# Bias tables moved into the first feed-forward, places kept for the first value weights, and a reordered begin of the second feed-forward in an f32 hybrid layer

## The chip, the core and the metric

One program on one core of a Trainium2 chip. The time is the device time of one launch in microseconds; a kernel's figure is the median over its runs. The profile of one launch is shown beside it.

## The reference

One layer on 1024 tokens of width 1024, all in float32:

```python
h = swiglu(rmsnorm(x, ffn1_pre_g), w_gate, w_up, w_down)      # width 2816
x = x + 0.5 * rmsnorm(h, ffn1_post_g)
q, k, v = split(rmsnorm(x, mix_pre_g) @ w_qkv)                # 16 heads of 64
o_na  = neighbourhood_attention(q[:8], k[:8], v[:8], na_rel_bias)   # windows on a 16 x 64 grid
o_dil = dilated_mixture_attention(q[8:], k[8:], v[8:], t5_rel_bias) # three dilated windows
x = x + rmsnorm(concat(rmsnorm(o_na), rmsnorm(o_dil)) @ w_out, mix_post_g)
h = swiglu(rmsnorm(x, ffn2_pre_g), ...)
x = x + 0.5 * rmsnorm(h, ffn2_post_g)
```

Both attentions add a bias to their scores: the first one from `na_rel_bias` by row and column offset, with a large negative number outside the window; the second from `t5_rel_bias` by a bucket of the distance.

## The kernel before, in words

The large products go by Strassen-Winograd: each operand is cut in four quarters, sums of quarters are formed, and seven products of half size take the place of eight. Each of them is three matmuls per 128 x 128 x 512 tile (lines 262 to 264), because a float32 operand is split into a high and a low fp32r part: high x high, high x low, low x high. A split is a cast on ACT (`pw` L612, `whi` L355) and a subtraction on DVE (L613, `wlo` L356).

`PairGemm` computes two weight blocks (gate and up, or q and k) against the normalised tokens. An "early" block needs only the first half of the tokens: `ahead` computes its products A11 and A12 and stores the sums to DRAM (s1d, sgd). Later `run` does the rest of every block, the full blocks: S2, the previous block's A22, S1, S3 and S4, twelve matmuls times five, with A11 and A12 first where the block had not been early. For each block DVE forms sums of the raw weights (L443 to L445, the steps direct and second of `prepare`), and ACT and DVE split them. `Passes` computes the products in seven passes over smaller pieces (the two down projections and the values); every `fetch` loads, casts and splits two pieces of weights.

The stages, in order: first feed-forward (early blocks to 100 us, full blocks to 460, down passes to 682), the first two value passes (to 716), early QK blocks (to 770), the other value passes (to 834), full QK blocks (to 940), attention (to 1175), w_out (to 1252), second feed-forward (early blocks to 1322, full blocks to 1690, down passes to 1900).

PE's order is written out by hand: the program's text is PE's order. `plan(n, {tick: [...]})` gives small steps to n turns, and a turn comes every six or twelve matmuls. Such a step is `U(t)`, the transposes of token tile t: four 128 x 128 transposes in one "put" on PE (`trp`, L170), then a cast on ACT (L171) and a subtraction on DVE (L172), with two buffers for trp. Five puts belong to a tile of the second half of the tokens, where sums of quarters (`s`, L234) are transposed too. `Finish.rest` loads the residual tiles (L732, from POOL's queue) and adds to them (L735); the norms follow (L162 on ACT, L211 on DVE). Most of the order on the other engines comes from a list scheduler; `c.behind(f, engines)` keeps what f issues behind the last instruction so far of the engines named. Every engine works through its queue in order, and SP and POOL issue most of the DMA transfers.

`build_bias` fills three tables in DRAM between the value passes: `gab` (two tables of 8 heads, each row shifted by one; L785), `nb` (filled with the negative number, L788, then with rows of the stacked bias, L793), from a small product with the bucket table (`tabp`, L780, with its addition L781 and its store `tab<-lc`, L782). The stacked bias `stk` is loaded at the program's start. Attention reads the tables.

## Time and profile before

| | |
|---|---|
| median of 3 runs | 1921.62 us (1916.37 to 1922.28) |
| the profiled execution | 1922.76 us, span 1921.0 us |
| mean granted TensorE clock | 0.989 |
| PE busy | 1851.7 us (96%) |
| DVE, ACT, POOL busy | 1313.9, 799.8, 311.7 us |
| DMA | 400.96 MB, mean 209 GB/s |

A row of the profile's groups reads: line, engine, operation, output <- inputs, shapes, count, then busy time and mean duration of one, then idle time of the engine just before, and what ended most of it. In a table of waits, "PE trp L170 <- DVE x L172: 4.3, 2, 2.6" says that PE's instruction of line 170 began late for DVE's line 172 by 4.3 us in all, twice, at most 2.6 us. In a timeline the row begins with start and duration, and ends with the idle time before the instruction and its releaser in brackets. PEclk is the granted clock as a share of full speed, and the DMA share is the mean busy share of 16 DMA engines.

### The profile page before, as it was taken

Reading aid. Unit: us, or ns where it says so; the run is one execution under the profiler, and the core shown is the slowest. Engines: PE = TensorE matmul, PEld = TensorE weight load, DVE = VectorE, ACT = ScalarE, POOL = GpSimd, SP = SyncE. Lnnn points to the kernel's source line nnn. Section 1 sums busy time; section 2 is a strip of 40 time slices with the busy share of each in tenths; the row PEclk is TensorE's granted clock in tenths of the full one; section 3 lists DMA queues with packets and bytes.
Section 4 is the critical chain, followed back from the end, with each engine's and each line's share of the span. In section 5 each row is a group of like instructions: output and inputs, shape, how many; then the busy total and the mean of one; then the engine's idle time right before and its main releaser. Section 6 shows DMA issues by size and latency. Waiting matters only on the chain.

```text
span 1921.0 us, 25047 instructions
## 1 busy us (share of the span) xinstructions
PE 1851.7 (96%) x9044; PEld 1545.2 (80%) x9044; DVE 1313.9 (68%) x2205; ACT 799.8 (42%) x1287; POOL 311.7 (16%) x504
## 2 busy tenths in 40 slices
PE   5999999999999989999999999989999999999997
PEld 4788888888888867778799987777888888888886
DVE  5778777676565866548566775776788777654557
ACT  4522333334444545224477765453222333344332
POOL 2111111111000122342432310121111111110000
PEclk8999999999999999999999999999999999999999
DMA  6645465645986756866974642483456655476563
GB/s 237 223 159 188 170 222 216 222 167 197 327 273 200 273 193 205 292 198 197 313 265 142 212 159 88 155 301 136 159 192 241 215 195 210 159 275 212 198 229 133
DMA packets 162461, 400.96 MB, mean 209 GB/s; under 512 B 18001, under 2 KB 34561, under 8 KB 160289
## 3 DMA queue, kind: packets, MB, share of 16 engines
q1 hardware_dynamic: 112880, 224.62, 35.3%
q0 software_dynamic: 48592, 172.64, 24.8%
q10 hardware_dynamic: 864, 2.10, 0.3%
q8 instruction: 71, 1.16, 0.2%
q14 instruction: 54, 0.43, 0.1%
HBM read 274.84 MB, written 129.50 MB: 210 GB/s over the span
## 4 chain that ended last, share of the span: by engine, by line
PE 82%; DVE 6%; issue 5%; DMA 4%; ACT 2%; POOL 1%; SPq 0%; DVEq 0%; POOLq 0%; ACTq 0%
PE mmp L264 16%; PE mmp L262 16%; PE mmp L263 16%; PE accp L263 8%; PE accp L262 8%; PE accp L264 8%; PE po L992 3%; PE ptp L891 2%; PE sp L980 2%; PE trp L170 1%; PE po L1113 1%; DMA wraw<-in_wqk_dram 1%; PE sp L1100 1%; DMA x<-x 1%; DMA wraw<-in_wu_dram 1%
## 5 line engine op out<-in xcount | busy, mean ns | idle before, releaser
L262 PE MATMUL mmp<-x,whi 128*128 128x512 f32 (+1 forms) x1464 | 579.8, 396 | 7.6 <-ACT whi L355 3.6
L264 PE MATMUL mmp<-x,wlo 128*128 128x512 f32 (+1 forms) x1464 | 575.5, 393 | 1.0 <-DVE wlo L356 1.0
L263 PE MATMUL mmp<-x,whi 128*128 128x512 f32 (+1 forms) x1464 | 574.8, 393 | 0.5 <-DVE x L172 0.2
L262 PEld LDWEIGHTS mmp<-x,whi 128*128 128x128 f32 x1464 | 278.2, 190 | 67.0 <-ACT whi L355 4.2
L264 PEld LDWEIGHTS mmp<-x,wlo 128*128 128x128 f32 x1464 | 277.9, 190 | 62.3 <-DVE wlo L356 1.9
L263 PEld LDWEIGHTS mmp<-x,whi 128*128 128x128 f32 x1464 | 278.4, 190 | 59.9 <-DVE x L172 1.4
L613 DVE TENSOR_TENSOR pw<-praw,pw 128x1024 fp32r<-128x1024 f32 (+1 forms) x182 | 199.2, 1138 | 122.4 <-ACT pw L612 122.1
L612 ACT CAST pw<-praw 128x1024 fp32r<-128x1024 f32 (+1 forms) x182 | 169.2, 983 | 208.6 <-PE accp L264 168.0
L355 ACT CAST whi<-wraw 128x1024 fp32r<-128x1024 f32 x129 | 135.2, 1050 | 251.6 <-PE mmp L263 213.0
L262 PE MATMUL accp<-pw 128*128 128x512 f32 x600 | 234.4, 391 | 0.0
L264 PE MATMUL accp<-pw 128*128 128x512 f32 x600 | 233.5, 389 | 0.0
L263 PE MATMUL accp<-pw 128*128 128x512 f32 x600 | 233.4, 389 | 0.0
L356 DVE TENSOR_TENSOR wlo<-wraw,whi 128x1024 fp32r<-128x1024 f32 x129 | 157.6, 1225 | 23.6 <-ACT whi L355 23.5
L264 PEld LDWEIGHTS accp<-pw 128*128 128x128 f32 x600 | 112.6, 188 | 23.7
L262 PEld LDWEIGHTS accp<-pw 128*128 128x128 f32 x600 | 112.7, 188 | 23.5 <-issue 0.4
L263 PEld LDWEIGHTS accp<-pw 128*128 128x128 f32 x600 | 112.7, 188 | 23.0
L560 POOL DMA_DIRECT2D g<-sg x44 | 23.9, 542 | 475.2 <-DVE sg L553 304.0
L518 DVE TENSOR_TENSOR c<-mmp,u 128x512 f32<-128x512 f32 x52 | 36.0, 691 | 83.9 <-PE mmp L264 82.8
L374 ACT COPY s<-mmp 128x512 f32<-128x512 f32 x52 | 30.5, 587 | 147.3 <-PE mmp L264 145.7
L355 ACT CAST whi<-traw 128x512 fp32r<-128x512 f32 x52 | 32.3, 621 | 118.2 <-DVE traw L444 59.2
L172 DVE TENSOR_TENSOR x<-trp,x 128x512 fp32r<-128x512 f32 x84 | 57.2, 687 | 34.7 <-ACT x L171 34.7
L443 DVE TENSOR_TENSOR wraw<-wraw 128x1024 f32<-128x1024 f32 x52 | 63.6, 1224 | 24.2 <-DMA wraw<-in_wqk_dram 11.9
(230 smaller groups left out, 2699.8 us busy)
## 6 DMA issues: line engine op xcount, KB each, us to landing
praw<-g SPq DMA_DIRECT2D x70, 512.0 KB
wraw<-in_wg_dram SPq DMA_DIRECT2D x44, 512.0 KB
wraw<-in_wu_dram SPq DMA_DIRECT2D x44, 512.0 KB
tr<-in_wd_dram SPq DMA_DIRECT2D x44, 512.0 KB
g<-sg POOLq DMA_DIRECT2D x88, 256.0 KB, 4.1
ts<-tr POOLq DMA_DIRECT2D x22, 1024.0 KB, 4.7
praw<-ts SPq DMA_DIRECT2D x88, 256.0 KB
praw<-in_wd_dram SPq DMA_DIRECT2D x66, 256.0 KB
```

The source lines that it names most:

```text
L172: nc.vector.tensor_sub(lo, ps, hi.bitcast(F32))
L262: nc.tensor.matmul(out, ahi, bhi, start=start, stop=False, skip_group_check=go_on)
L263: nc.tensor.matmul(out, ahi, blo, start=False, stop=False, skip_group_check=go_on)
L264: nc.tensor.matmul(out, alo, bhi, start=False, stop=stop, skip_group_check=go_on)
L355: nc.scalar.copy(hi, raw)
L356: nc.vector.tensor_sub(lo, raw, hi.bitcast(F32))
L443: nc.vector.tensor_sub(r[:, 0:2], r[:, 1:3], r[:, 0:2])
L612: nc.scalar.copy(w[side][:, 0, :m], raw[:, :m])
L613: nc.vector.tensor_sub(w[side][:, 1, :m], raw[:, :m], w[side][:, 0, :m].bitcast(F32))
L891: c.nc.tensor.transpose(self.tps[:, j, :], self.probs[:, j * P:(j + 1) * P], c.ident)
L980: nc.tensor.matmul(out, lhs, keys[i], start=i == 0, stop=i == 1)
L992: nc.tensor.matmul(po[0][:, un * 2 + j], u.pt[:, 2 * j + t, :], rhs, start=t == 0, stop=t == 1)
```

## The change

Six things are done.

1. `build_bias` becomes `bias_steps`: the same tables, in pieces that are spread over the turns 0 to 19 of the first feed-forward's full blocks, one to six transfers a turn. `gab` goes by head (16 pieces of 256 KB), the filling of `nb` in 4 pieces of 384 KB; the loads of `stk` leave the program's start and come here too. Each step is held behind the last POOL and DVE instruction.
2. The first value pass has a place of its own (pool `pf`) and raw buffers (pool `pv`) that exist during the last down passes: its first weights are loaded at turn 13 there, and cast and split at turn 20. The first two passes take their pieces in groups of two rather than four, with a turn every six matmuls. Four tiles `vt` stand in place of two.
3. The early QK blocks 0, 3 and 6 take that place for their split weights, and their raw loads the same raw buffers. The split of block 0 is issued at turn 13 of the 16 turns of these value passes.
4. In the value passes behind the early QK blocks, the first weights of the full QK blocks are loaded and prepared one pass further back, behind the last DVE and ACT instructions so far.
5. In the full blocks that had been early, `direct` and `second` for the next block are held behind u of this block on DVE.
6. The second feed-forward has 11 early blocks instead of 10; the transposes of tiles 0 and 1 come one turn earlier; the split of the first early block is issued with the last turns of w_out, into a place in the residual tiles' pool.

The core of the diff (lines left out are marked by "..."):

```diff
@@ -402,13 +409,16 @@
...
-            if b + 1 not in self.w:
+            later = b == 1 and 3 in self.place
+            if b + 1 not in self.w and not later:
...
+            if later:
+                c.behind(lambda: self.split_left(b + 1), ACT, DVE)
...
@@ -479,10 +489,10 @@
                 self.mm(a, w[T2], 0, S2)
                 u2 = sp.tile([P, T], F32, tag="u2", name="u2")
                 nc.vector.tensor_add(u2, a, s1)
+                marks = c.marks(DVE, ACT)
                 if last:
                     last()
-                direct()
-                second()
+                c.after(marks, lambda: (direct(), second()))
                 a = self.bank()
                 self.mm(a, w[T1], 0, S1)
                 v = sp.tile([P, T], F32, tag="v", name="v")
@@ -584,29 +594,44 @@
...
+    def __init__(self, c, n, left, right, take, last=None, first=None):
...
-        self.groups = [groups] * 6 + [last or groups]
+        self.groups = [first or groups] * 2 + [groups] * 4 + [last or groups]
...
             self.groups[0] = [groups[0][:2], groups[0][2:]] + groups[1:]
         self.todo = deque((p, g[j:j + 2]) for p in range(7) for g in self.groups[p] for j in range(0, len(g), 2))
...
+        self.ready, self.places, self.loaded, self.raws = deque(), deque(), deque(), None
+    def load(self, raw):
+        p, ids = self.todo[len(self.loaded)]
+        for j, i in enumerate(ids):
+            self.c.nc.sync.dma_start(raw[:, j], self.right(i)[PASSES[p][1]])
+        self.loaded.append(raw)
...
+        p, ids = self.todo[0]
...
+        if self.places:
+            w = [self.places.popleft()()]
+            if not self.loaded:
+                self.load(self.raws.tile([P, 2, T], F32, tag="raw", name="praw"))
+        self.todo.popleft()
...
+            loaded = bool(self.loaded)
+            raw = (self.loaded or raws).popleft() if self.loaded or raws else c.pw.tile([P, 2, T], F32, tag="raw",
+                                                                                       name="praw")
...
+            elif not loaded:
...
@@ -763,35 +788,65 @@
...
+def bias_steps(c, rel, t5, onehot, lncount, bp):
+    nc, g = c.nc, c.nc.gpsimd
...
+    def load(i):
...
+        g.dma_start(kept["oh"][:32, :511], onehot[:, cols])
+        g.dma_start(kept["lc"][:8, :511], lncount[:, cols].broadcast_to([8, 511]))
+    def begin():
+        c.bp = bp()
...
+        g.dma_start(kept["t5"], t5.rearrange("h b -> b h"))
...
+        g.memset(kept["neg"], NEG)
+        load(0)
+    def table(i):
+        oh, lc = kept["oh"], kept["lc"]
...
+        g.dma_start(tab[i, :, :511], lc[:8, :511])
+        if i == 0:
+            load(1)
+    def shift(h, i):
...
+        dst = bass.AP(tensor=x.tensor, offset=x.offset + h * P * 640, ap=[[641, P], [1, 511]])
+        g.dma_start(dst, tab[i, h:h + 1, :511].broadcast_to([P, 511]))
+    def fill(h):
+        g.dma_start(c.nb[h:h + 2].rearrange("h p r e -> p h (r e)"),
+                    kept["neg"].unsqueeze(1).broadcast_to([P, 2, 384]))
+    def shifted(cc):
+        g.dma_start(stk[cc], rel[:, :, 7 - cc:31 - cc])
+    def rows(r):
...
+        g.dma_start(c.nb[:, r * 8:r * 8 + 8, r0:r0 + 8, :].rearrange("h c r e -> c h (r e)"),
+                    stk[:, :, r0 - r + 7:r0 - r + 15, :].rearrange("c h r e -> c h (r e)"))
+    at = {0: [begin], 1: [lambda: table(0)], 2: [lambda: table(1)]}
...
+    for n in range(4):
+        add(n, fill, 2 * n)
+    for n in range(8):
+        add(n + 1, shifted, n)
+        for i in range(2):
+            add(2 * n + i + 4, shift, n, i)
+            add(n + 9, rows, 2 * n + i)
+    return {k: [lambda f=f: c.behind(f, POOL, DVE) for f in fs] for k, fs in at.items()}
...
@@ -1237,8 +1292,8 @@
...
-        def one_a_turn(steps, n, first):
-            plan(n, {first + i: [f] for i, f in enumerate(steps)})
+        def one_a_turn(steps, n, first, more):
+            plan(n, {i: steps[i - first:i - first + 1] * (i >= first) + more.get(i, []) for i in range(n)})
...
@@ -1284,11 +1340,13 @@
...
-            one_a_turn(sums, NF, NF - 3 - len(sums))
+            bt = sub()
+            one_a_turn(sums, NF, NF - 3 + (which == 3) - len(sums), tables(pool, bt))
...
+                bt.close()
...
@@ -1329,7 +1387,7 @@
...
-                          9: [lambda: fin.rest([2, 3], hs.get)], 10: [U(1)], 17: [U(2)], 19: [U(3)]})
+                          9: [lambda: fin.rest([2, 3], hs.get)], 10: [U(1)], 17: [U(2)], 19: [U(3)], **tail(prep, op)})
...
@@ -1415,34 +1473,57 @@
...
+            def values_ahead(stack, op):
+                vp.append(Passes(c, 4, op, getv, vearly, first=[[0, 1], [2, 3]]))
...
+                def place():
+                    return first.tile([P, 1, 2, 2, T], F32R, tag="w", name="pw")[:, 0]
+                def load():
...
+                    vp[0].places.append(place)
...
+                    for i in range(2):
+                        vp[0].load(raws.tile([P, 2, T], F32, tag="raw", name="praw"))
+                return {13: [load], 20: [lambda: vp[0].fetch()]}
+            op, fin, hs, prep = ffn(1, op0, prep, gate_pairs(1, op0, a["wg1"], a["wu1"], 9), get1,
+                                    {0: [F(4, 5), L(6, 7)], 2: [U(4)], 3: [F(6, 7), U(5)], 5: [U(6)], 6: [U(7)]},
+                                    down_sums(a["wd1"], ts1), value_sums(a["wv"], tsv),
+                                    a["ffn1_post_g"], a["mix_pre_g"], x0, x1, begin,
+                                    lambda pool, e: bias_steps(c, a["na_rel_bias"], a["t5_rel_bias"], a["onehot"],
+                                                               a["lncount"], lambda: pool("bp", 1, e)), values_ahead)
+            qkv, w, e = sub(), sub(), sub()
+            c.xb = pool("xb", 1, qkv)
+            op.second()
+            vp, = vp
+            pr, c.vt = pool("pr", 2, e), pool("vt", 1, e)
+            vp.places.extend([lambda: pr.tile([P, 1, 2, 2, T], F32R, tag="w", name="pw")[:, 0]] * 3)
+            for i in range(4):
+                vts.append(c.vt.tile([P, 4 * VW], F32, tag=f"v{i}", name="vt"))
+                nc.gpsimd.memset(vts[i].rearrange("p (h f) -> p h f", f=65)[:, :, 64:65], 1.0)
...
+            pg.place = {b: lambda: early[0]().rearrange("p h m x -> h p m x") for b in (0, 3, 6)}
+            plan(16, {0: [lambda: fin.scale(4, 4), A(4, 5)], 9: [lambda: queued(pg.start)], 10: [U(4)],
+                      13: [lambda: c.behind(lambda: pg.split_left(0), DVE, ACT)]})
...
+            early_pools(e, 2, 2)
...
@@ -1460,12 +1540,12 @@
...
-            pg.fetch(0)
-            pg.fetch(1)
-            build_bias(c, a["na_rel_bias"], a["t5_rel_bias"], a["onehot"], a["lncount"])
-            vp.run(4, 5)
-            pg.begin()
-            pg.begin_rest()
+            queued(lambda: pg.fetch(0))
+            vp.run(4)
+            queued(lambda: pg.fetch(1))
+            c.behind(pg.begin, DVE, ACT)
+            vp.run(5)
+            c.behind(pg.begin_rest, DVE, ACT)
...
@@ -1600,7 +1680,9 @@
             p2, g3 = prep_pool(prep, [(a["mix_post_g"], "post"), (a["ffn2_pre_g"], "pre")])
             left_pool(prep, side="right")
             op = Operand(c, g3, 2)
-            pg = gate_pairs(3, op, a["wg2"], a["wu2"], 10)
+            pg = gate_pairs(3, op, a["wg2"], a["wu2"], 11)
+            pg.place[0] = lambda: c.xp.tile([P, 2, 2, T], F32R, tag="s", name="w0", bufs=c.deep).rearrange(
+                "p h m x -> h p m x")
             fin = Finish(c, x1, x2, p2, op)
             hs = [part, hs1p.tile([P, 4, D], F32, name="hs")]
             A = lambda *ts: lambda: fin.rest(ts, lambda t: hs[t // 4][:, t % 4, :])
@@ -1621,8 +1703,8 @@
...
-            plan(12, {0: [lambda: fin.scale(0, 4), A(0, 1)], 3: [A(2, 3)], 5: [U(0)], 6: [U(1)],
-                      8: [lambda: queued(pg.start)], 9: [U(2)], 10: [U(3)]})
+            plan(12, {0: [lambda: fin.scale(0, 4), A(0, 1)], 3: [A(2, 3)], 4: [U(0)], 5: [U(1)],
+                      7: [lambda: queued(pg.start)], 9: [U(2)], 10: [U(3), lambda: pg.split_left(0)]})
...
```

Three places show how the order moves. First, DVE at full QK blocks 0 and 1 (`u` and `c` with the lower numbers are block 0's). Before:

```order
L481 TENSOR_TENSOR u_6581<-mmp,s_6566 128x512
L356 TENSOR_TENSOR wlo<-traw,whi 128x512
L444 TENSOR_TENSOR traw<-wraw 128x512
L445 TENSOR_TENSOR wraw<-wraw,traw 128x512
L489 TENSOR_TENSOR v<-mmp,u_6581 128x512
L356 TENSOR_TENSOR wlo<-wraw,whi 128x1024
L481 TENSOR_TENSOR u_6659<-mmp,s_6644 128x512
L356 TENSOR_TENSOR wlo<-traw,whi 128x512
L510 TENSOR_TENSOR c_6618<-mmp,v 128x512
L810 TENSOR_TENSOR k<-mmp,u_6581 128x512
```

With the change:

```order
L491 TENSOR_TENSOR u_6587<-mmp,s_6572 128x512
L453 TENSOR_TENSOR wraw<-wraw 128x1024
L454 TENSOR_TENSOR traw<-wraw 128x512
L455 TENSOR_TENSOR wraw<-wraw,traw 128x512
L499 TENSOR_TENSOR v<-mmp,u_6587 128x512
L363 TENSOR_TENSOR wlo<-traw,whi 128x512
L520 TENSOR_TENSOR c_6624<-mmp,v 128x512
L363 TENSOR_TENSOR wlo<-wraw,whi 128x1024
L865 TENSOR_TENSOR k<-mmp,u_6587 128x512
L890 TENSOR_TENSOR qk<-k,qk 128x512
L491 TENSOR_TENSOR u_6665<-mmp,s_6650 128x512
L453 TENSOR_TENSOR wraw<-wraw 128x1024
```

The first c has moved from behind the second u to ahead of it, and the preparation (L443 before, L453 now) of the next weights stands behind u.

Second, POOL in the first two value passes (`vs` and `v` are where the values are stored, `x` the residual tiles). Before, the load of tiles 6 and 7 and what stands ahead of it:

```order
L1436 DMA vs_5324<-vt 128x520
L1433 MEMSET vt 128x8
L1436 DMA vs_5324<-vt 128x520
L1433 MEMSET vt 128x8
L732 DMA x<-in_x_dram 128x1024 x2
L1070 DMA v_87<-vt 8x8x520 x2
```

With the change:

```order
L1516 MEMSET vt 128x8 x4
L220 DMA xn_2_4842<-xn 128x1024
L220 DMA xn_3_4843<-xn 128x1024
L757 DMA x<-in_x_dram 128x1024 x2
L761 DMA x_4_97<-x 128x1024
L761 DMA x_5_98<-x 128x1024
L1483 DMA vs_163<-vt 128x520 x4
L757 DMA x<-in_x_dram 128x1024 x2
```

The fills of vt with ones are all ahead of the first store; the loads of tiles 6 and 7 (the last row) stand behind the four stores of the first pass, as before.

Third, DVE at the end of the early blocks of the second feed-forward, where the last tiles are transposed (L172 before, L178 now). Before:

```order
L172 TENSOR_TENSOR x_11247<-trp,x_11246 128x4x128
L137 TENSOR_SCALAR v<-ss 128x2
L443 TENSOR_TENSOR wraw<-wraw 128x1024
L138 TENSOR_SCALAR y<-v 128x2
L172 TENSOR_TENSOR x_11239<-trp,x_11238 128x4x128
L139 TENSOR_SCALAR y<-y 128x2
L356 TENSOR_TENSOR wlo<-graw,whi 128x1024
L146 TENSOR_TENSOR e<-y,v 128x2
L172 TENSOR_TENSOR x_11241<-trp,x_11240 128x4x128
L147 TENSOR_TENSOR e<-e,y 128x2
L172 TENSOR_TENSOR x_11243<-trp,x_11242 128x4x128
```

With the change:

```order
L240 TENSOR_TENSOR s<-x_11811,s 128x512
L178 TENSOR_TENSOR x_11258<-trp,x_11257 128x4x128
L178 TENSOR_TENSOR x_11250<-trp,x_11249 128x4x128
L178 TENSOR_TENSOR x_11252<-trp,x_11251 128x4x128
L178 TENSOR_TENSOR x_11254<-trp,x_11253 128x4x128
L178 TENSOR_TENSOR x_11256<-trp,x_11255 128x4x128
L453 TENSOR_TENSOR wraw<-wraw 128x1024
L454 TENSOR_TENSOR traw<-wraw 128x512
L455 TENSOR_TENSOR wraw<-wraw,traw 128x512
```

The preparation of the first full block stood among the subtractions of the last two tiles; now it stands behind all of them.

87 lines of the change are left out of this document (32 added, 55 removed).

## The prediction

> **What bounds the kernel now.** I read the page's engine shares first, then stretches of the span with PE's busy time and granted clock, then PE's waits in the three stretches where it is short, then the rows of the engines that it waits for.
>
> ```profile
> PE 1851.7 (96%) x9044; PEld 1545.2 (80%) x9044; DVE 1313.9 (68%) x2205; ACT 799.8 (42%) x1287; POOL 311.7 (16%) x504
> ```
>
> The next engine, DVE, is busy for 68%; PE sets the time, with 1851.7 of the 1921.0 us. The diff keeps its matmuls, so it can win only the 69 us in which PE is idle and the stretches in which its clock is low. The stretches (span, PE busy, ..., clock, DMA share):
>
> ```profile
> core 0: us, PE busy (x) PEld busy (x) DVE busy (x) ACT busy (x) POOL busy (x), PEclk, DMA share, GB/s
> 100.00:240.00 140.00, 140.00 (x613) 114.99 (x613) 110.68 (x147) 35.34 (x44) 17.79 (x32) 1.00 0.53 175
> 682.00:728.00 46.00, 35.79 (x161) 26.60 (x160) 30.86 (x59) 21.76 (x36) 12.46 (x27) 1.00 0.62 213
> 810.00:818.00 8.00, 7.29 (x20) 5.79 (x21) 3.46 (x5) 0.00 (x0) 1.15 (x3) 0.59 1.02 250
> 850.00:854.00 4.00, 4.00 (x13) 3.09 (x12) 1.15 (x2) 1.46 (x2) 1.54 (x2) 0.59 0.31 99
> 1294.00:1298.00 4.00, 3.70 (x13) 3.03 (x14) 3.79 (x14) 0.60 (x2) 0.00 (x0) 0.57 0.43 128
> 1318.00:1326.00 8.00, 6.52 (x23) 5.37 (x24) 5.58 (x9) 1.76 (x3) 0.00 (x0) 0.57 0.23 82
> ```
>
> In the first row, full gated blocks, PE has no gap, so there is nothing to win there and something to lose. The second loses 46.00 - 35.79 = 10.2 us at full clock. In the other four PE runs at little over half clock; busy time times (1 - clock) is what that costs: 7.29 x 0.41 = 3.0, 4.00 x 0.41 = 1.6, 3.70 x 0.43 = 1.6 and 6.52 x 0.43 = 2.8 us. Each follows a gap. PE's waits in three windows (682 to 728, 806 to 855, 1235 to 1326; us in total, times, longest):
>
> ```profile
> PE trp L170 <- DVE x L172: 4.3, 2, 2.6
> PE accp L263 <- DVE pw L613: 2.0, 3, 1.0
> PE mmp L262 <- ACT whi L355: 1.7, 1, 1.7
> PE accp L262 <- ACT pw L612: 1.5, 2, 0.8
> PE mmp L264 <- DVE wlo L356: 0.5, 1, 0.5
> ...
> PE accp L263 <- DVE pw L613: 3.0, 1, 3.0
> PE mmp L262 <- DVE c L510: 2.0, 1, 2.0
> ...
> PE trp L170 <- DVE x L172: 8.6, 6, 3.4
> PE mmp L262 <- ACT whi L355: 1.8, 1, 1.8
> PE mmp L264 <- DVE wlo L356: 0.5, 1, 0.5
> ```
>
> Sums: A, first value passes, 10.0. B, end of the value passes and first two QK blocks, 5.0 and clock 3.0 + 1.6: 9.6. C, w_out to the end of the second feed-forward's early blocks, 10.9 and clock 1.6 + 2.8: 15.3. Together 34.9 us, all in the reach of the diff. The start, the turn into attention and the tail hold the other half of the idle time; the diff leaves them.
>
> **A, first value passes.** What PE waits for, on DVE, ACT and POOL:
>
> ```profile
> 703.10 1.09 POOL L732 DMA_DIRECT2D x<-in_x_dram  x2 [0.73 <-DVE s L234]
> 707.22 1.28 DVE L735 SCALAR_TENSOR_TENSOR x<-hb,y,x 128x1024 f32<-128x1024 f32 x1 [3.44 <-DMA x<-in_x_dram]
> 711.34 0.66 PE L170 MATMUL trp<-ident,s 128*128 128x128 f32 x4
> 697.27 0.59 ACT L1434 COPY vt<-accp 128x512 f32<-128x512 f32 x1 [3.04 <-DMA vs<-vt]
> ```
>
> The weight waits (2.0 + 1.5) have two reasons: the first pair is split only when the down passes have ended, and ACT's next cast stands behind a copy into vt that waits 3.04 us for a store, since vt has two buffers. Now the first pair has places of its own and is cast during the last down pass, half of a pass's weights is enough to begin, and four vt tiles end the copy's wait. I take 3.5 off. The QK split (1.7 + 0.5) stands behind the last copy of the passes; it moves to turn 13 of 16, with its load behind a raw buffer that comes free at the second split, some 20 us ahead of need. 2.2 off, 0.4 kept, as its two casts and subtractions end close to PE's arrival.
>
> The waits for a transposed tile (2.6, 1.8) are DVE's subtraction L172 behind L735, which waits for tile 6's load. In the new order the first subtraction is ahead of that addition, but the second is behind it. So the fourth transpose is gated where the third was. It arrives about 706.7: 711.34 before, less the 6.0 us of stalls ahead of it (3.5 for weights, 2.6 for the third transpose), plus six matmuls (140.00 us over 613, 0.23 each). The load goes 0 to 2.5 us before 703.10, as the two weight splits, about 1.2 us each, no longer stand before its release; it landed 4.1 us after issue (707.22), and 1.28 for the addition and 0.7 for the subtraction follow, so the tile is free between 706.7 and 709.2. That keeps 0 to 2.5 us; I take the middle, 1.3, having no row nearer to either end. The 1.8 had a split behind a late load ahead of it, which now lands earlier: 0.3 kept. A: **10.0 less 2.0 = 8.0** (4.9 where 2.5, 1.8 and 0.8 stay, 9.3 where no tile is waited for).
>
> **B, bias tables out of the value passes.** DVE here, with the DMA issues of 770 to 840 (KB each, us to landing):
>
> ```profile
> gab<-tab POOLq DMA_DIRECT2D x2, 2044.0 KB, 19.0
> nb<-neg POOLq DMA_DIRECT2D x1, 1536.0 KB, 8.3
> tab<-lc POOLq DMA_DIRECT2D x2, 16.0 KB, 6.8
> ...
> 807.09 1.23 DVE L443 TENSOR_TENSOR wraw<-wraw 128x1024 f32<-128x1024 f32 x1 [5.89 <-DMA wraw<-in_wqk_dram]
> 809.43 1.22 DVE L613 TENSOR_TENSOR pw<-praw,pw 128x1024 fp32r<-128x1024 f32 x1
> 847.58 0.69 DVE L481 TENSOR_TENSOR u<-mmp,s 128x512 f32<-128x512 f32 x1 [3.38 <-PE mmp L264]
> 848.78 0.68 DVE L510 TENSOR_TENSOR c<-mmp,v 128x512 f32<-128x512 f32 x1
> ```
>
> L443 waits 5.89 us for gated weights that share the engines (share 1.02) with 5.6 MB of bias; the split L613 that PE needs is queued behind it. Now the bias is gone from here and L443 stands behind four of the last splits, so either change alone would free PE. The 2.0 us gap is c of block 0 queued behind u of block 1, which waits 3.38 us for a product PE had yet to make; in the new order c is ahead. I keep 0.5 for the shorter queue. B: **9.1** (3.6 where the first gap and its clock, 6.0, stay; 9.6 where nothing does).
>
> What the bias costs in its new place: two small matmuls and additions, moved with PE's sum unchanged; the loads have one block of 13.7 us (60 matmuls) for landings of which the longest here, at a full DMA, was the 6.8 of tab. One chain is longer: the second lc load waits for the first tab store, so DVE's second addition may stand 0 to 2 us. PE would see that only past the slack of 3.1 us worked out under the slower rival; I charge 0.3. The pieces are one to six a block and hold POOL about half a microsecond each (x32 in 17.79 us of the 140), and their 6.4 MB over 20 blocks of at least 13.7 us are under 25 GB/s, at a DMA share of 0.53. What hides them is PE's own queue of products; were that cover gone, a block would be as much longer as its slowest piece is late.
>
> **C, second feed-forward's begin.** DVE and PE rows, the last from the first feed-forward:
>
> ```profile
> 1228.77 2.48 DVE L211 SCALAR_TENSOR_TENSOR xn<-x,y,gain 128x1024 f32<-128x1024 f32 x2
> 1231.73 0.60 PE L170 MATMUL trp<-ident,xn 128*128 128x128 f32 x4
> 1292.34 1.23 DVE L443 TENSOR_TENSOR wraw<-wraw 128x1024 f32<-128x1024 f32 x1 [4.05 <-DMA wraw<-in_wu_dram]
> 86.58 0.66 PE L170 MATMUL trp<-ident,s 128*128 128x128 f32 x4 [1.07 <-DVE x L172]
> ```
>
> The 10.9 are 1.5 at the transposes of U0 and U1 near 1237 and 1239, 2.3 at the first split, 3.4 at 1294 and 3.7 at the last seven puts (1316 to 1321). U0 goes one turn (12 matmuls, 2.75 us) earlier: it arrives about 1229.0, and the first half of L211 ends at 1230.0, so 1.0 to 1.1 us of wait takes the place of 1.5. The first split is placed two thirds into the last w_out turns instead of behind them: 2.3 off. L443 no longer stands before the last transposes: 3.4 and its clock loss of 1.6 off. An eleventh early block gives the seven puts that ended in a burst six matmuls each, all but the last three; a burst of three is what the first feed-forward ends with, and it waits 1.07. So of 3.7 + 2.8, 1.1 stays. C: **15.3 less 2.2 = 13.1** (7.7 where the burst and its clock stay, 14.2 where the last three puts wait for nothing). The eleventh block saves no matmul; its extra store and reload are 1 MB off PE's path.
>
> **Sum.** 8.0 + 9.1 + 13.1 - 0.3 = 29.9 off the profiled execution's 1922.76 us gives 1892.9; the median of the runs is 1.1 lower than that execution, so 1891.8: **1892 us**. The three low ends (16.2, less 0.3) give 1906, the high ones (33.1) 1888; the start, where eight small loads leave POOL ahead of the first tiles' stores, I put at nothing.
>
> The clock terms rest on rows: clock 0.59 behind gaps of 3.0 and 2.0 us, though the 2.6 us gap of A left it at 1.00. [...]
>
> **The rivals.** *The stalls pass on*: tile 6's load and the splits stay gates. Then A keeps 4.3 + 2.2, and C keeps its burst's 3.7 + 2.8 because transposes that come earlier find DVE just as full: 13.0 against the 3.1 that I keep there, so 1902. For it: most of the waits above name a subtraction queued on DVE, which is left 68% busy. Against it: behind 2.6, 3.0 and 3.4 of them stands a DMA wait (3.44, 5.89, 4.05) whose instruction is moved. *The loads are late without the bias too*, as the DMA share stays 1.02 in the row of 810 to 818, where the pieces of bias are only a part: B keeps its first gap and clock, 3.0 + 3.0, hence 1898. Against: 5.6 MB leave, and L443 stands further back. [...] *The change doesn't act*, schedulers refilling what is won: within 5 us of 1921.
>
> *Slower: DVE's new order in the early full blocks.* The preparation of the next weights (L443 and two more) was hoisted ahead of u; now it is held directly behind u, ahead of c and of the split needed three products later.
>
> ```profile
> 105.89 1.22 DVE L443 TENSOR_TENSOR wraw<-wraw 128x1024 f32<-128x1024 f32 x1
> 109.42 0.68 DVE L481 TENSOR_TENSOR u<-mmp,s 128x512 f32<-128x512 f32 x1
> ...
>   DMA wraw<-in_wu_dram: 11.4, 9
> ```
>
> From the end of u's product: u 0.7, the preparation 1.2 + 0.7 + 0.7, c 0.7, the split 1.2 (as L613 above): 5.2 us, against three products of 12 matmuls, 36 x 0.23 = 8.3, to the one that needs it. Slack 3.1. A DMA wait in front of L443 now hits that split, and cancels the gain if it costs PE 29.9 / 28 = 1.07 us in each of the 28 early full blocks, a wait of 4.2 us; at 4.7 us the time is 1892 + 28 x 1.6 = 1937. For it: DVE is busy 110.68 of 140. Against it: L443 moves 4 us later (behind 109.42 + 0.68, from 105.89), and in its early place it waited 11.4 us in all for these loads, 4.05 of them at 1292.
>
> **How the numbers follow.** My forecast 0.60 (its own range 1886 to 1899), stalls pass on 0.18, loads late 0.08, clock 0.03, doesn't act 0.06, slower 0.05. The range 1885 to 1909 takes in the first four and the low ends, with 3 us at either side for what the sum leaves out. A measurement tells 0.3% (6 us) from no change: faster 0.89, same 0.06, slower 0.05.
>
> **What would show it.** PE without waits over 0.5 us and clock 1.00 from 790 to 850 (B); one wait of about 1 us at a transpose in A, and two of about 1 us in C; no 8 us stretch of clock 0.57 before the second gated blocks; PE without idle time in the early full blocks. Idle time there, or a wait of DVE for wraw in every block, would be the slower rival; a 2 us wait for c, or half clock near 810, proves my B wrong.

## The result, and the profile after

The changed kernel takes **1899.96 us** in the median of four runs (1898.66 to 1901.49), the kernel before, timed beside it, 1921.95 (1916.37 to 1922.31). The ratio is 0.9899, with a 95% interval of 0.9877 to 0.9921; by the medians it is faster by 22.0 us, where 29.9 were forecast. The profiled execution took 1899.15 us (span 1897.0, mean granted clock 0.994), 23.6 less than that of before.

PE's line of the page, and the six stretches of the prediction's first table, after:

```profile
PE 1842.2 (97%) x9044; PEld 1538.3 (81%) x9044; DVE 1316.3 (69%) x2207; ACT 794.9 (42%) x1285; POOL 320.7 (17%) x519
```

```profile
core 0: us, PE busy (x) PEld busy (x) DVE busy (x) ACT busy (x) POOL busy (x), PEclk, DMA share, GB/s
682.00:728.00 46.00, 43.04 (x206) 34.39 (x205) 36.73 (x76) 24.30 (x44) 12.24 (x22) 1.00 0.63 211
810.00:818.00 8.00, 8.00 (x37) 6.64 (x36) 5.39 (x6) 2.95 (x3) 3.21 (x7) 1.00 0.38 117
850.00:854.00 4.00, 4.00 (x19) 3.33 (x18) 3.93 (x7) 1.57 (x2) 0.84 (x2) 1.00 0.71 201
1294.00:1298.00 4.00, 4.00 (x23) 3.32 (x22) 4.00 (x7) 2.32 (x5) 1.08 (x2) 1.00 0.17 66
1318.00:1326.00 8.00, 8.00 (x37) 6.54 (x36) 5.74 (x9) 1.67 (x2) 0.54 (x1) 1.00 0.43 154
100.00:240.00 140.00, 138.36 (x599) 111.51 (x599) 110.97 (x148) 34.65 (x44) 30.66 (x55) 1.00 0.59 196
```

The first row lost 10.2 us before and loses 46.00 - 43.04 = 3.0 now. The four stretches at half clock are gone. Only the last row is worse: PE had no gap in the early full blocks and now has one. PE's waits after, from the windows 100 to 460, 455 to 682, 678 to 735, 1205 to 1326 and 1440 to 1480 (us in total, times, longest); the window 806 to 855 has none:

```profile
PE mmp L268 <- DVE v L499: 1.6, 1, 1.6
...
PE accp L269 <- DVE pw L638: 1.0, 2, 0.6
...
PE mmp L270 <- DVE wlo L363: 1.7, 1, 1.7
PE trp L176 <- DVE x L178: 1.3, 1, 1.3
...
PE trp L176 <- DVE x L178: 2.5, 4, 1.3
PE trp L176 <- DVE xn L217: 0.9, 1, 0.9
...
PE mmp L268 <- DVE v L499: 2.5, 1, 2.5
```

What is left of A is 1.7 + 1.3 = 3.0, of B nothing, of C 2.5 + 0.9 = 3.4. Two places are new: a wait for `v` in each feed-forward, 1.6 + 2.5 = 4.2 us, and 1.0 us in the first feed-forward's down passes. So A won 10.0 - 3.0 = 7.0, B 9.6 and C 15.3 - 3.4 = 11.9, and 4.2 + 1.0 went back: 23.3 of the 23.6 us by which the profiled executions differ. The miss to be explained is the new waits (the two for `v` and those of the down passes), and some 2 us of more waiting in A and C than was allowed.

### The profile page after: what moved, and what is told of

It is laid out like the page before. It is cut to its first block, busy times and chain, and to the rows that moved or that the text cites. A ratio compares the mean times of both kernels' runs of the same rounds, so it can differ in the third digit from the quotient of the medians.

```text
span 1897.0 us, 25061 instructions
## 1 busy us (share of the span) xinstructions
PE 1842.2 (97%) x9044; PEld 1538.3 (81%) x9044; DVE 1316.3 (69%) x2207; ACT 794.9 (42%) x1285; POOL 320.7 (17%) x519
## 4 chain that ended last, share of the span: by engine, by line
PE 84%; DVE 6%; DMA 4%; issue 3%; ACT 2%; POOL 0%; SPq 0%; DVEq 0%; ACTq 0%; POOLq 0%
PE mmp L268 16%; PE mmp L270 16%; PE mmp L269 16%; PE accp L269 8%; PE accp L268 8%; PE accp L270 8%; PE po L1047 3%; PE ptp L946 2%; PE sp L1035 2%; PE trp L176 1%; PE po L1168 1%; PE sp L1155 1%; DMA tsv<-tr 1%; DMA sgd<-sg 1%; DMA gain<-in_ffn_pre_g_dram 0%
## 5 line engine op out<-in xcount | busy, mean ns | idle before, releaser
L268 PE MATMUL mmp<-x,whi 128*128 128x512 f32 (+1 forms) x1432 | 565.8, 395 | 6.5 <-DVE v L499 4.2
L270 PE MATMUL mmp<-x,wlo 128*128 128x512 f32 (+1 forms) x1432 | 561.2, 392 | 1.7 <-DVE wlo L363 1.7
L269 PE MATMUL mmp<-x,whi 128*128 128x512 f32 (+1 forms) x1432 | 560.7, 392 | 0.5 <-DVE x L178 0.2
L268 PEld LDWEIGHTS mmp<-x,whi 128*128 128x128 f32 x1432 | 271.1, 189 | 67.2 <-issue 6.5
L270 PEld LDWEIGHTS mmp<-x,wlo 128*128 128x128 f32 x1432 | 271.0, 189 | 61.0 <-DVE wlo L363 2.4
L269 PEld LDWEIGHTS mmp<-x,whi 128*128 128x128 f32 x1432 | 271.3, 189 | 58.0 <-DVE x L178 1.4
L270 PEld LDWEIGHTS accp<-pw 128*128 128x128 f32 x600 | 112.6, 188 | 23.6
L178 DVE TENSOR_TENSOR x<-trp,x 128x512 fp32r<-128x512 f32 x84 | 57.3, 687 | 38.7 <-ACT x L177 38.6
L177 ACT CAST x<-trp 128x512 fp32r<-128x512 f32 x84 | 48.8, 586 | 53.1 <-PE trp L176 52.7
L453 DVE TENSOR_TENSOR wraw<-wraw 128x1024 f32<-128x1024 f32 x52 | 63.5, 1221 | 0.8
```

Of the source, the lines that this page charges most:

```text
L177: nc.scalar.copy(hi, ps)
L178: nc.vector.tensor_sub(lo, ps, hi.bitcast(F32))
L268: nc.tensor.matmul(out, ahi, bhi, start=start, stop=False, skip_group_check=go_on)
L269: nc.tensor.matmul(out, ahi, blo, start=False, stop=False, skip_group_check=go_on)
L270: nc.tensor.matmul(out, alo, bhi, start=False, stop=stop, skip_group_check=go_on)
L453: nc.vector.tensor_sub(r[:, 0:2], r[:, 1:3], r[:, 0:2])
```

## The experiments

The table lists every kernel with its median, its ratio to the kernel before (timed on the same chip), and two sums of its own profile from 40 us on: PE's idle gaps over 0.3 us, and busy time times (1 - granted clock) in stretches of 2 us with a clock under 0.97; the second also holds the program's first 40 us. "The hold" is item 5 of the change; u, v and c (L491, L499 and L520 in the changed kernel) are DVE's additions behind a block's products S2, S1 and S3.

| kernel | median us | ratio [95%] | PE idle | clock |
|---|---|---|---|---|
| before | 1921.95 | | 35.1 | 14.5 |
| the change | 1899.96 | 0.9899 [0.9877, 0.9921] | 21.3 | 5.9 |
| e1, hold in early blocks only | 1895.58 | 0.9861 [0.9843, 0.9878] | 18.9 | 4.4 |
| e2, no hold | 1903.31 | 0.9902 [0.9887, 0.9916] | 24.0 | 7.7 |
| e3, bias tables back | 1904.58 | 0.9905 [0.9891, 0.9920] | 23.8 | 9.1 |
| e5, bias tables and preparation back | 1903.81 | 0.9905 [0.9890, 0.9919] | 22.4 | 9.1 |
| e6, ten early blocks | 1901.76 | 0.9890 [0.9868, 0.9912] | 20.7 | 11.9 |
| e7, first split where it was | 1898.88 | 0.9879 [0.9865, 0.9894] | 19.4 | 10.4 |
| e8, all of A back | 1902.87 | 0.9906 [0.9884, 0.9928] | 19.8 | 9.1 |
| e9, e1 and sums one turn later | 1894.43 | 0.9855 [0.9838, 0.9873] | 15.5 | 8.2 |
| e10, e9 and the second split first | 1893.06 | 0.9845 [0.9830, 0.9860] | 12.6 | 5.6 |
| e11, U0 and U1 a turn later | 1901.54 | 0.9887 [0.9871, 0.9903] | 21.7 | 6.8 |
| f1, before with the hold alone | 1916.38 | 0.9978 [0.9963, 0.9993] | 28.3 | 12.7 |
| f2, before with the bias moved alone | 1915.64 | 0.9966 [0.9951, 0.9982] | 26.9 | 13.6 |

An interval is some 3 to 4 us to each side. The last column also moves without any edit's doing: of it, 2.8 to 5.8 us fall in the first 60 us and 1.4 to 3.0 at the turn into attention (near 940), and kernels whose programs are the same there differ as much. The kernels that undo one part (e2, e3, e5 to e8, e11) all overlap with the change, so their times alone prove nothing; what follows from them rests on which gaps come and go in their traces. e9 and e10 lie wholly below the change's interval, f1 and f2 wholly above it.

**The wait for v: e1.** The hold is kept where the next block is early too, and left out otherwise.

```diff
-                c.after(marks, lambda: (direct(), second()))
+                if b + 1 < self.early:
+                    c.after(marks, lambda: (direct(), second()))
+                else:
+                    direct()
+                    second()
```

> The changed kernel, but the preparation of the next block is held behind u only where that next block is an early one too; at the last early block of each feed-forward the order is the scheduler's again. My theory: PE's two waits for v (1.64 us near 217 and 2.52 us near 1459) come from the hold, because the next block there is not an early one, so its preparation carries one more split, and all of it stands ahead of v on DVE. Then both waits go and the time falls by about 4 us, to 1896. Rival: the waits come from what else DVE has there (the sums for the down passes, the bias tables' additions): then they stay, and the time stays within 1 us of 1900.

DVE in the changed kernel, in the last early full block (the second u) and in the one two blocks ahead of it:

```profile
180.25 0.69 DVE L491 TENSOR_TENSOR u<-mmp,s 128x512 f32<-128x512 f32 x1 [1.38 <-PE mmp L270]
186.98 0.68 DVE L499 TENSOR_TENSOR v<-mmp,u 128x512 f32<-128x512 f32 x1
...
207.67 0.69 DVE L491 TENSOR_TENSOR u<-mmp,s 128x512 f32<-128x512 f32 x1 [1.38 <-PE mmp L270]
208.28 1.22 DVE L363 TENSOR_TENSOR wlo<-wraw,whi 128x1024 fp32r<-128x1024 f32 x1
...
216.63 0.69 DVE L499 TENSOR_TENSOR v<-mmp,u 128x512 f32<-128x512 f32 x1
```

From u to v it is 6.7 us in the earlier block and 9.0 in the last. The next block of the last is no early one, so its `direct` also splits the first half of its weights (208.28, 1.22 us), and the hold puts this ahead of v with all the rest. v is ready 1.6 us late, and PE's next product needs it: it adds to the bank that v reads. In e1 the gap at 217 is gone, and PE waits for nothing over 0.3 us from 100 to 460. At the same place of the second feed-forward the 2.5 us are gone too, but two others came, 0.95 us for a cast at 1453 and 1.86 us at 1469, behind this row of DVE:

```profile
1464.82 1.23 DVE L333 TENSOR_TENSOR tr<-tr 128x1024 f32<-128x1024 f32 x1 [7.04 <-DMA tr<-in_wd_dram]
```

That is a sum for the down passes, issued in the same turns, whose load is late; behind it stands DVE's part of the block, for which ACT waits 5.38 us, and PE waits for ACT's copy behind that. Idle time fell from 21.3 to 18.9 us, the median by 4.4; 0.9 of that is a shorter stretch of half clock at the turn into attention, which the edit doesn't touch. In the first feed-forward the wait for v is the hold at one block: all eight kernels with the full hold have it (1.64 us), and none of the six others. In the second it isn't the hold alone. With the hold and ten early blocks (e6 and f1, below) it is absent, and e2, with eleven blocks and no hold, still waits 1.38 us for v there and 1.22 at 1477.

**The sums out of the way: e9.** e1, and the second feed-forward's sums one turn later.

```diff
-            one_a_turn(sums, NF, NF - 3 + (which == 3) - len(sums), tables(pool, bt))
+            one_a_turn(sums, NF, NF - 3 + 2 * (which == 3) - len(sums), tables(pool, bt))
```

> The hold only where the next block is an early one too, and in the second feed-forward the sums for the down passes one turn later, so that none of them stands on DVE beside the last early block. In the run with the hold alone 0.95 and 1.86 us were lost there. If those sums are the reason, both go and the time is 1893; if the last early block is too full for DVE without them too, 1 us or more stays at v, u or a split, and the time is within 1 us of 1895.6.

Measured 1894.43, and PE has no wait between 1440 and 1480 any more. So in the second feed-forward the loss goes when the hold and the sums are both taken out of the last early block; the sums moved with the hold left in were not run.

**What the hold is good for: e2 and f1.** e2 is the change without the hold; f1 is the kernel before with only the hold put in.

```diff
-                c.after(marks, lambda: (direct(), second()))
+                direct()
+                second()
```

> The changed kernel without any hold of the preparation behind u. If the hold is what put c ahead of the next block's u in the first full QK blocks, PE's wait of 2.0 us for c and the low clock behind it (1.6 us) come back near 840, and the two waits for v (4.2 us) go: within 1 us of the changed kernel. If c moved for another reason (its data are simply earlier now, since the weights are), there is no wait for c, and the time falls by 4 us to 1896.

f1, in the kernel before:

```diff
...
-                direct()
-                second()
+                with ExitStack() as st:
+                    for i in marks:
+                        st.enter_context(c.tc.issue_after(i))
+                    direct()
+                    second()
```

> The kernel before with only the hold of the next block's preparation behind u. If the hold is what frees PE at 810 and at 1294, those two gaps and their low clock go (3.0 + 3.0 and 3.4 + 1.6), the wait for c near 849 stays or grows to 4 us with 3 us of clock (as in the runs with the bias tables back), and the last early block may cost 1.6 in the first feed-forward and up to 2.5 in the second: 1914 to 1919. If the bias transfers are what holds PE at 810, that gap stays: 1919 to 1922.

PE in e2, the DVE row behind which its operand stood, and the window 790 to 800 (columns as in the stretches above):

```profile
791.67 0.50 PE L269 MATMUL accp<-pw,x 128*128 128x512 f32 x1 [2.87 <-DVE pw L639]
```

```profile
789.25 1.23 DVE L453 TENSOR_TENSOR wraw<-wraw 128x1024 f32<-128x1024 f32 x1 [4.03 <-DMA wraw<-in_wqk_dram]
...
1275.08 1.23 DVE L453 TENSOR_TENSOR wraw<-wraw 128x1024 f32<-128x1024 f32 x1 [3.86 <-DMA wraw<-in_wu_dram]
```

```profile
790.00:800.00 10.00, 8.33 (x30) 6.69 (x30) 4.73 (x6) 0.00 (x0) 2.06 (x4) 0.83 0.43 139
```

Though the bias tables are gone from here and the first block's own preparation stands further back (804.39), the next block's preparation stands in the value passes again (789.25), waits 4.03 us for its load, and PE's split waits behind it: 2.87 us and 8.33 x 0.17 = 1.4 us of clock. At 1275 the same happens, and PE waits 3.36 us for a transposed tile at 1277, as it did for 3.39 at 1294 before. So of the two outcomes expected of e2 neither came whole: there is no wait for c, yet the median rose by 3.4 us. f1 has neither gap, with the bias tables where they were and no other part of the change: PE's one wait from 786 to 855 is that for c, shown below. Its median is 4.4 us under the kernel before, inside what was expected.

**The wait for c: e3, e5, f2.** e3 builds the bias tables between the value passes again, in the changed kernel; e5 also takes back item 4, the place of the full QK blocks' first preparation; f2 is the kernel before with only the bias moved.

```diff
...
-                                    lambda pool, e: bias_steps(c, a["na_rel_bias"], a["t5_rel_bias"], a["onehot"],
-                                                               a["lncount"], lambda: pool("bp", 1, e)), values_ahead)
+                                    lambda *x: {}, values_ahead)
...
             queued(lambda: pg.fetch(0))
+            c.bp = pool("bp", 2, e)
+            build_bias(c, a["na_rel_bias"], a["t5_rel_bias"], a["onehot"], a["lncount"])
             vp.run(4)
```

> The changed kernel with the bias tables built in the value passes again; the preparation of the first full QK weights stays held further back. As predicted, either of the two alone frees PE at 810: then there is no 3 us wait and no half clock there, and the time is within 2 us of 1900. Rival: the transfers themselves are what counts (the DMA share of 1.02), so loads of value weights or of gated weights are late whatever DVE's order is: a wait of 3 us or more and low clock between 780 and 850, 1905 to 1908.

e5 has these lines in place of the passes' as well:

```diff
-            queued(lambda: pg.fetch(0))
-            vp.run(4)
-            queued(lambda: pg.fetch(1))
-            c.behind(pg.begin, DVE, ACT)
-            vp.run(5)
-            c.behind(pg.begin_rest, DVE, ACT)
+            pg.fetch(0)
+            pg.fetch(1)
...
+            vp.run(4, 5)
+            pg.begin()
+            pg.begin_rest()
```

> The changed kernel with both undone, bias tables and the preparation of the first full QK weights back in the value passes as before the change. This brings back the whole first half of part B: a wait of about 3 us at a value pass and about 3 us of clock, 1906 together with what else was seen there. If part B's gain came from elsewhere (earlier arrival, the hold), it stays near 1900.

f2 is the other way round, put into the kernel before: `build_bias` out, `bias_steps` in the first feed-forward's turns.

> The kernel before, with the bias tables moved into the first feed-forward and nothing else of the change. My prediction gave this move the whole of part B's first half (3.0 us of wait and 3.0 of clock): about 1915. The theory from the first four runs is the other way round: the wait for the split at 810 is a matter of the hold and stays (2.9 to 3.0 us, half clock behind it), while the wait for c (2.0 us and 1.6 of clock) goes, since c stands ahead of u only where the bias transfers are gone: 1917 to 1919, with one gap near 810 and none near 849.

PE's waits from 786 to 855 in f1, and in f2:

```profile
PE mmp L262 <- DVE c L514: 4.0, 1, 4.0
```

```profile
PE accp L269 <- DVE pw L639: 1.0, 1, 1.0
```

In e3 DVE shows the order, and the window PE's loss:

```profile
834.12 0.69 DVE L491 TENSOR_TENSOR u<-mmp,s 128x512 f32<-128x512 f32 x1 [3.31 <-PE mmp L270]
...
837.31 0.68 DVE L520 TENSOR_TENSOR c<-mmp,v 128x512 f32<-128x512 f32 x1
```

```profile
836.00:844.00 8.00, 5.95 (x15) 4.71 (x16) 4.69 (x7) 2.50 (x3) 1.54 (x2) 0.57 0.45 141
```

Wherever the tables are built in the value passes (before, e3, e5, f1), c stands behind the second u, and with the hold behind the preparation as well: 2.0 us before, 3.97 in the three others. In e3 that is 3.97 us and 5.95 x 0.43 = 2.6 of clock. Where the tables are elsewhere (the change, e2, f2), c is ahead and PE waits for nothing there. No gap at 790 to 820 is in e3, e5 or f1. So the hold by itself frees the value passes, and the bias move frees c. A preparation that waits there need not cost anything: in e5 the first block's, which the hold doesn't touch, waits 3.75 us for its load, and PE waits for nothing from 720 to 830.

```profile
780.58 1.23 DVE L453 TENSOR_TENSOR wraw<-wraw 128x1024 f32<-128x1024 f32 x1 [3.75 <-DMA wraw<-in_wqk_dram]
```

The bias move does part of the hold's job too. f2 shortened the first gap (3.0 to 1.0 us, L453 waiting 0.34 instead of 5.89) and has no half clock there, but did not end it; its median of 1915.6 is the 1915 of my prediction, and not the 1917 to 1919 of the later theory, which kept that gap whole. Why the tables' presence turns the order of u and c is a decision of the program's scheduler that no run here opened. f2 shows as well what the pieces cost in their new place: it has no gap between 87 and 685 us.

**A: e8.** First value passes and early QK blocks as before, all else changed.

```diff
...
+            c.pr, c.pw, c.vt = pool("pr", 3, e), pool("pw", 2, e), pool("vt", 2, e)
...
-            def values_ahead(stack, op):
-                vp.append(Passes(c, 4, op, getv, vearly, first=[[0, 1], [2, 3]]))
...
-                return {13: [load], 20: [lambda: vp[0].fetch()]}
...
+            vp = Passes(c, 4, op, getv, vearly)
...
-            pg.place = {b: lambda: early[0]().rearrange("p h m x -> h p m x") for b in (0, 3, 6)}
-            plan(16, {0: [lambda: fin.scale(4, 4), A(4, 5)], 9: [lambda: queued(pg.start)], 10: [U(4)],
-                      13: [lambda: c.behind(lambda: pg.split_left(0), DVE, ACT)]})
+            plan(8, {0: [lambda: fin.scale(4, 4), A(4, 5)], 4: [U(4)], 5: [lambda: queued(pg.start)]})
```

> The changed kernel with the first value weights' places, the four vt tiles, the groups of two and the early QK blocks' places taken back, so that part A is as before the change. By the prediction's rows this costs 10.0 less the 3.0 us that the changed kernel still loses there: 1907, with weight waits of 3.5 us, 2.3 at the first QK split and 4.3 at transposes. Rival: the waits are passed on, since only their places move: within 3 us of 1900. The wait of about 1 us near 575, new in the changed kernel, should go if it comes from the early value loads on SP's queue.

PE's waits from 678 to 735 in e8, and one of its windows:

```profile
PE mmp L268 <- ACT whi L362: 1.7, 1, 1.7
PE accp L269 <- DVE pw L638: 1.0, 1, 1.0
PE mmp L270 <- DVE wlo L363: 0.5, 1, 0.5
PE accp L268 <- ACT pw L637: 0.5, 1, 0.5
PE trp L176 <- DVE x L178: 0.5, 1, 0.5
```

```profile
688.00:694.00 6.00, 5.17 (x15) 3.87 (x16) 5.50 (x17) 2.15 (x5) 0.00 (x0) 0.72 0.57 196
```

Undoing A costs 2.9 us in the median, not 7 or 8: 4.2 us of waits and, by the last row, a stretch of low clock behind the first two, 5.17 x 0.28 = 1.4, stand in place of the 3.0 above and of the 1.0 in the down passes. e8's trace also has half clock behind the wait for v near 1461, which costs up to 1.7 and which the changed kernel's has not. The first weight wait (1.5) and the QK split's (2.2) are back, as they should be. The second weight wait (1.4 before) and the 2.6 us for a transposed tile are not: DVE's addition that gates the tile waited 3.44 us for its load before, and 0.81 at the same place (707.79) here. So part of what A seemed to win came from elsewhere in the change. f1 has none of A's edits either: its waits from 678 to 735 are 4.9 us instead of 10.0, the second weight wait and the later of the two tile waits (1.8 us) among those that are gone. But it has two stretches of half clock of 3.41 us there (687.59 and 718.31), some 3 us of clock that the kernel before doesn't have, so most of that is taken back. Which part of the change brings the load in earlier is open.

**A's own new wait: e10.** e9, and the split of QK block 1 issued ahead of the plan, the four sums of the next tile held behind it on DVE.

```diff
...
+            pg.split_left(1)
+            c.hold = c.marks(DVE)
             plan(8, {0: [A(6, 7), U(5)], 3: [U(6)], 5: [U(7)]})
+            c.hold = None
```

> The kernel with the hold only beside early next blocks and the sums one turn later, and with the second early QK block's split ahead of the next tile's sums of quarters on DVE. PE waits 1.7 us for that subtraction near 718, as the four sums (2.4 us) stand before it. If the queue's order is the reason, the wait goes and nothing takes its place, as the sums are needed 2 us later: 1893. If the split is late for its cast on ACT, the wait stays at 1 us or more: 1894.4.

DVE in the changed kernel before the 1.7 us wait of PE at 719.79, and in e10:

```profile
715.52 0.68 DVE L240 TENSOR_TENSOR s<-xn 128x512 f32<-128x512 f32 x1
...
717.92 0.68 DVE L240 TENSOR_TENSOR s<-x,s 128x512 f32<-128x512 f32 x1
718.52 1.22 DVE L363 TENSOR_TENSOR wlo<-graw,whi 128x1024 fp32r<-128x1024 f32 x1
```

```profile
712.28 1.23 DVE L364 TENSOR_TENSOR wlo<-graw,whi 128x1024 fp32r<-128x1024 f32 x1 [0.26 <-ACT whi L363]
713.42 0.68 DVE L241 TENSOR_TENSOR s<-xn 128x512 f32<-128x512 f32 x1
```

The split stood behind all four sums of a tile whose products come later. Counted from the addition of the last tile (711.98 and 707.19), it now begins 5.1 us later instead of 6.5. What is left of A's 3.0 us is 0.41 and 0.37, at other matmuls. The 1.4 us between e9 and e10 are less than their intervals, so that this wait was the queue's order rests on the traces. e10's median is 1893.06, 6.9 us below the change and some 28 below the kernel before (ratio 0.9845): **it beats both**.

**C: e6, e7, e11.** Ten early blocks again, and with them the second feed-forward's sums for the down passes, which the change had moved one turn later, in their old turns; the first early block's split not issued at turn 10; U(0) and U(1) at turns 5 and 6 again.

```diff
-            one_a_turn(sums, NF, NF - 3 + (which == 3) - len(sums), tables(pool, bt))
+            one_a_turn(sums, NF, NF - 3 - len(sums), tables(pool, bt))
...
-            pg = gate_pairs(3, op, a["wg2"], a["wu2"], 11)
+            pg = gate_pairs(3, op, a["wg2"], a["wu2"], 10)
```

```diff
-            plan(12, {... 4: [U(0)], 5: [U(1)], ... 10: [U(3), lambda: pg.split_left(0)]})
+            plan(12, {... 4: [U(0)], 5: [U(1)], ... 10: [U(3)]})
```

```diff
-            plan(12, {... 4: [U(0)], 5: [U(1)], ...
+            plan(12, {... 5: [U(0)], 6: [U(1)], ...
```

> The changed kernel with 10 instead of 11 early blocks in the second feed-forward; all else is kept, the hold too. If the eleventh block is what took away the burst of seven puts, 3.7 us of wait and 2.8 of low clock come back near 1300, less the 1.3 that is left: 1905. If the hold alone did it (DVE is no longer late there), the burst costs 2 us or less and full clock stays: 1901.

> The changed kernel with the first split of the second feed-forward's early blocks issued behind w_out's last turns again. By the prediction the 2.3 us of waits for the cast and the subtraction come back near 1235: 1902. If the place alone frees the split (the scheduler may begin it early without being told), within 1 us of 1900.

> The changed kernel with the transposes of tiles 0 and 1 in the second feed-forward's preparation at turns 5 and 6 again. By the prediction 1.0 us of wait for the norm turns back into 1.5 us of waits for subtractions behind the residual additions: within 1 us of 1900. Rival: the later turn crowds what follows it (the first split, the first puts of the early blocks) and costs 2 us or more.

e6's PE at the end of the early blocks, and its window of 1300 to 1307:

```profile
1295.98 0.63 PE L176 MATMUL trp<-ident,xn 128*128 128x128 f32 x4 [1.48 <-DVE x L178]
1298.90 1.29 PE L176 MATMUL trp<-ident,s 128*128 128x128 f32 x8 [1.69 <-DVE x L178]
1300.95 1.11 PE L176 MATMUL trp<-ident,s 128*128 128x128 f32 x4 [0.77 <-DVE x L178]
```

```profile
1300.00:1307.00 7.00, 6.23 (x19) 4.94 (x18) 4.53 (x6) 1.34 (x3) 0.00 (x0) 0.51 0.47 179
```

The burst is back almost to the tenth: 3.9 us of waits and 6.23 x 0.49 = 3.1 of clock, against 1.3 with eleven blocks. Yet the median is only 1.8 us higher. With ten blocks the second feed-forward has no wait for v at all, though the hold is in: in the last early block the program's scheduler now puts the later steps of the preparation (L454 and what follows it) behind v.

```profile
1441.51 1.22 DVE L453 TENSOR_TENSOR wraw<-wraw 128x1024 f32<-128x1024 f32 x1
1442.64 0.68 DVE L499 TENSOR_TENSOR v<-mmp,u 128x512 f32<-128x512 f32 x1
1443.25 0.68 DVE L454 TENSOR_TENSOR traw<-wraw 128x512 f32<-128x512 f32 x1
```

So the eleventh block wins the burst, and together with the hold it brings the wait of 2.5. In e7 PE's waits from 1205 to 1260 are the 0.92 for xn and nothing else, so the first split is on time without being issued at turn 10: the place of its own is enough. In e11 the two turns cost 2.2 us at the transposes (1.22 and 0.98) where 0.92 stood: 1.3 us, and the median is 1.6 higher.

**The down passes.** The two waits near 575 us were no one's target. SP's waits from 555 to 600 in the changed kernel have this row:

```profile
SPq L612 <- DVE pw L638: 7.5, 1, 7.5
```

On SP's queue a load of value weights, new among the last down passes, stood 7.5 us for a split, with the down passes' own loads behind it. In e8, which has no such load, PE has no wait there, which fits. But e5 and e10 have the load (it stood 4.8 and 6.3 us) and no wait over 0.3 us, and in e8 the down passes' own loads stand for splits as well, 7.8 us at the longest. The cause of the 1 us is not settled.

## Why the prediction was right or wrong

**Direction and range** held: 1900 lies between 1885 and 1909. The forecast of 1892 was 8 us low, just outside its own range of 1886 to 1899. The working took the median as 1.1 us under the profiled execution, where it was 0.8 above this time: some 2 of the 8. The other 6 are terms: the two waits for v (4.2) and the down passes' 1.0, for which the sum had nothing, A's 1.0 and C's 1.2, less 0.5 from B and the 0.3 charged for lc.

**A, 8.0 kept, 7.0 measured.** The weight waits (3.5) went, as worked out. The one wait of about 1.3 us at a transposed tile came (1.25), though DVE's addition ahead of it waits for another tile's load, so that the size is partly luck. The step that failed is the "0.4 kept" and "0.3 kept" for splits: block 0's split is on time, but moving block 1's put it behind four sums, for 1.7 us. And e8 shows that I credited A with too much: with A undone 4.2 us of waits and 1.4 of clock are lost there, not 10.0. The 2.6 us for the third transpose and the second weight wait are gone in e8, without A's edits.

**B, 9.1 kept, 9.6 measured**; the size is right and the cause only in part. "Either change alone would free PE" at 810 failed. With the bias gone and L443's first preparation moved, e2 still waits 2.87 us; with the bias in place and only the hold, f1 waits for nothing. What mattered was whether the next block's preparation stands in the queue of the passes, and that is the hold's doing, the edit that I had weighed only as a danger. The c term is the other way round: I gave it to the new order, and it comes with the bias move. The 0.3 for lc measured nothing (no gap in f2).

**C, 13.1 kept, 11.9 measured.** U0's wait (1.0 to 1.1 foreseen) is 0.92, the burst's rest (1.1) is 1.34, and the 3.4 at 1294 is gone, by the hold as e2 and f1 show. The first split's 2.3 are gone too, but by its place and not by its turn (e7). Not foreseen are three waits of 0.3 to 0.5 us at transposes between 1262 and 1277, together 1.1.

**The rivals.** "The stalls pass on" did not come: the transposes that now come earlier find DVE free enough. "Loads late without the bias too" fell in the changed kernel, where 810 to 818 shows a DMA share of 0.38; but its mechanism is in e2: a DMA share of 0.51 from 784 to 790, and still 4.03 us of waiting for the load there. So the load was late there without a full DMA. The clock's 0.03, half clock that stays although the gaps go, fell with the four stretches, which went with their gaps (0.57 to 0.59 before, 1.00 after); so did "doesn't act". The **slower rival had the right mechanism and the wrong place**: work held behind u delays what PE needs, but not in 28 blocks by a late load. It does so in the two blocks at which early ones end, and it has no need of a load there. The failed step is "5.2 us against ... 8.3": I counted the preparation of an early next block in every case, and left v and the block's own combinations out of the queue. From the start of u to the end of v it is 7.4 us in the earlier block and 9.65 in the last, where a split of 1.2 us is added and two more combinations get ahead of v; only the second is over the 8.3. In the second feed-forward the eleventh block and the sums have a share in it. The two waits are 4.2 of the missing 6 us. e1 gives back the 1.6, and in place of the 2.5 has 2.8 of other waits; e9 gives back both.

## What to carry to other kernels

When work is held behind a mark in a loop, walk through the block at which the kinds of iteration change: the same call does more there, and its price is that of the largest case. In e2 and in e5 an addition on DVE waited for its load (4.03 and 3.75 us) with other work queued behind it. That cost PE 2.87 us in e2 and nothing in e5, where the work behind it was not yet needed; where there is no such slack, keep such a wait out of a queue that feeds PE, and know that moving other transfers away to make its load faster was the weaker cure here (of the 3.0 us at 810, f2 left 1.0 and f1 nothing). Prices of waits read off one trace need not add up when parts are undone one by one: undoing A, the eleventh block, the hold and the bias move costs 2.9 + 1.8 + 3.4 + 4.6 = 12.7 us by the medians, each uncertain by 3 to 4, and all together won 22.
